# Two layers on one core: the merges' buffers and low parts, the last projection's banks, small matmuls of S5 and SSD, and how S5's time steps are loaded

## The chip, the core and the metric

The kernel runs on one core of a Trainium2 chip. The core has five engines with instruction streams of their own: TensorE (PE; its weight loads are listed as PEld), VectorE (DVE), ScalarE (ACT), GpSimd (POOL) and SyncE (SP), whose queue starts most DMAs here. The metric is the time of one execution on the device in microseconds; the figure to beat or miss is the median of three runs. A profiled execution gives the trace from which all rows below are taken.

## The reference, cut to what matters

The program computes two layers over 1024 tokens of width 1024, each of which projects its normalised input to three mixers and three gates, and merges the mixers' outputs.

```python
# layer 1: mixers S5 (a), mLSTM (b), sparse attention (c), each 512 wide
proj = rmsnorm(x, norm_g) @ w_in
y_a = s5_mixer(u_a, ...) * silu(z_a); y_b = mlstm(...) * silu(z_b); y_c = dsa(...) * silu(z_c)
branch = einsum('blnw,nwd->blnd', stack([y_a, y_b, y_c], 2), w_branch)
x1 = rmsnorm(x + sum(sigmoid(gate_pre) * branch, axis=2) @ w_out, final_norm_g)
# s5_mixer, 32 groups of 16 channels with 64 complex states each
dt = exp(log_dt)[:, None];  abar = exp(ar * dt) * (cos(ai * dt) + 1j * sin(ai * dt))
h[t] = abar * h[t - 1] + (bbar @ u[t]);  y = real(c @ h) + d_skip * u
# layer 2: stick-breaking attention (512), SSD (1024), RWKV-7 (512), merged in the same way
y_diag = einsum('bclgn,bcsgn,bcgjls,bcsgjp->bclgjp', cm, bm, decay_in, x_dt)     # SSD, chunks of 128
y_off = einsum('bclgn,bcgjpn,bcgjl->bclgjp', cm, prev_states, exp(a_cs))
out = rms_norm(x1 + sum(gate * (y @ w_out_i)) @ w_o, final_g)
```

## The kernel before

All tiles hold channels on the 128 partitions and tokens along the row. The large products are in three parts: each fp32 operand is split into a high part (a ScalarE copy to the engine's rounded fp32 type) and a low part (the rest, by VectorE or GpSimd), and `mm3` issues high x high, high x low and low x high as three matmuls of 128x128 by 512 columns, 0.227 us apart at the full clock. `proj` does one output tile of 128 channels in two halves of 512 tokens, each with a PSUM bank `pp` of its own (two banks in turn), and then calls an evacuation.

The order on each engine is fixed when the program is built: the scheduler of the tile framework lays out the instructions of all stages along its own time line, and each engine then runs its stream in order. Projections that a later stage needs (`ahead`: gates and values of the mixers, weights `fhi`/`flo`, written to DRAM through `fs`) are laid as fillers between the small matmuls of the recurrent stages.

Layer 1 runs norm, S5, sparse attention, mLSTM, merge, output projection with the norm of layer 2. Layer 2 runs the stick-breaking attention, SSD, RWKV-7, merge, output projection.

S5 (`s5`) reads its parameters, among them the 32 time steps, into `s5_dt` (two groups of 64 partitions by 16), takes their exponential (L583), and makes powers of the transition on VectorE. Then it goes through four channel tiles `ct`: the projection `uT` (evicted by ScalarE at L717), a convolution with a kernel `KK` of eight steps, held as the Toeplitz tile `Tz`, and a carry over blocks of eight tokens, a scan on VectorE that ends in `wr`/`wi`. The output of each of eight groups is Tz by U (128 rows) plus Vr by wr and Vi by wi (64 rows each, the upper or the lower half of the partitions), added up in PSUM.

SSD goes through eight chunks; for each half j of the heads it multiplies `xd` by `aB` (the part inside the chunk) and the state `S` by `bc` (the part from before).

A merge (`merge_branch`) goes through branches. `merge_y` loads the mixer's output y (and, where it is still to be gated, z), multiplies and splits it into the high and low tile in `hT[0]`. For each of eight output tiles d and each half, `eb` loads the gate `sg`, and VectorE multiplies it with the projection's bank (L425); GpSimd adds it to `acc` (L426). In layer 1 the branches run in the order a, c, b; in layer 2 four calls do attention, the two halves of SSD, and RWKV. The last branch does one half of the tokens after the other: behind its eight tiles, ScalarE writes the high part of the sum into `hT[0]` (L434) and VectorE the low part into `ml` (L435). `out_norm` then takes 128 tokens at a time: two PSUM banks `on` of 24 matmuls each, the residual `on_x` added by VectorE (L471), and the final norm.

The buffers of a merge are in one pool with two buffers a name: y has four, z two, the gate two; in layer 2 z takes the gate's.

Of the kernel before, what the change touches and what calls it, by code (L numbers as in the profile page):

```python
# [8 lines left out]
F32 = mybir.dt.float32  # L9
# [6 lines left out]
OP = mybir.AluOpType  # L16
# [93 lines left out]
def layout(i):  # L110
# [15 lines left out]
    o["s5_ldt"] = i["ssm_log_dt"][0]  # L126
# [52 lines left out]
class Kernel:  # L179
# [211 lines left out]
    def merge_y(self, p2, ysrc, zname, ztag, halves, here):  # L391
# [18 lines left out]
    def merge_branch(self, p2, first, last, acc, ysrc, zname, wb, base, gate, between=None, ml=None,  # L410
                     here=None, ztag="mg_z"):
# [3 lines left out]
        for halves in ((0,), (1,)) if last else ((0, 1),):  # L415
            y = self.merge_y(p2, ysrc, zname, ztag, halves, here)
            for d in range(8):
                def eb(half, ps):
                    t = slice(512 * half, 512 * half + 512)
                    sg = p2.tile([128, 512], F32, name="mg_s")  # L420
                    SP.dma_start(sg, self.done[f"{gate}_{d}"][:, t])
                    if first:
                        V.scalar_tensor_tensor(acc[:, d, t], sg, 1.0, ps, op0=OP.add, op1=OP.mult)
                    else:
                        V.scalar_tensor_tensor(sg, sg, 1.0, ps, op0=OP.add, op1=OP.mult)  # L425
                        self.G.tensor_tensor(acc[:, d, t], acc[:, d, t], sg, op=OP.add)  # L426
# [25 lines left out]
    def out_norm(self, ml, ws, res, g_dram, sm, done):  # L452

        tc, V, A, SP = self.tc, self.V, self.A, self.SP
        with self.pool(name="on", bufs=1) as pg, self.pool(name="on2", bufs=2) as p2, \
                self.pool(name="onp", bufs=2, space=PSUM) as pp:
# [22 lines left out]
    def block1(self):  # L479
# [3 lines left out]
        with ExitStack() as top:  # L483
# [59 lines left out]
            with self.pool(name="mw", bufs=2, side="right") as self.wp, \  # L543
                    self.pool(name="mg2", bufs=2, side="right") as p2:
# [19 lines left out]
            self.out_norm(ml, ws, I["x"], I["final_norm_g"], so, done)  # L564

    def s5(self, es):
# [129 lines left out]
        for ct in range(4):  # L696
# [60 lines left out]
            kks = [self.pm.tile([128, 4, 16], F32, name="pm") for _ in range(2)]  # L757
            for j in range(4):
                for g2 in range(2):
                    r = slice(64 * g2, 64 * g2 + 64)  # L760
                    self.mm(kks[g2][:, j], WTr[r, j].rearrange("p s q -> p (s q)"),
                            P["cr"][r, 4 * ct + j], True, False)
                    self.mm(kks[g2][:, j], WTi[r, j].rearrange("p s q -> p (s q)"),
                            nci[r, 4 * ct + j], False, True)
# [38 lines left out]
            yps = [self.pm.tile([128, 4, 128], F32, name="pm") for _ in range(2)]  # L803
            for j in range(4):
                for g2 in range(2):
                    g, ps = 2 * j + g2, yps[g2]
                    r = slice(64 * g2, 64 * g2 + 64)
# [521 lines left out]
    def block2(self):  # L1329
# [3 lines left out]
        with ExitStack() as top:  # L1333
# [36 lines left out]
            with self.pool(name="mw2", bufs=2, side="right") as self.wp, \  # L1370
                    self.pool(name="mg4", bufs=2, side="right") as p2:
# [737 lines left out]
```

## Time and profile before

| what | value |
|---|---|
| runs | 2820.71, 2817.85, 2813.22 us; median 2817.85 |
| profiled execution | 2822.19 us, span 2820.2, mean granted clock 0.977 |
| TensorE | 2687.4 us busy, 95% |
| VectorE, ScalarE, GpSimd | 1758.6 (62%), 1140.9 (40%), 660.9 us (23%) |
| DMA | 324.85 MB, 115 GB/s on average |

The profile is one execution. The span is the time from the first to the last instruction, and 2 us of the execution lie around it. The granted clock is TensorE's, 1 for 2.4 GHz and 0.5 for 1.2 GHz. In the rows, names are cut (`s_dt` for `s5_dt`, `hl` for the tile that is `acc` in a merge, since they share a buffer), and one fp32 matmul that is not split is two instructions.

### The profile page before, as it was taken

The numbers are of one execution on the slowest core, as the hardware profiler recorded it, in microseconds if no ns is written. First come the engines' busy times: TensorE is split into PE (matmuls) and PEld (weight loads), VectorE is DVE, ScalarE is ACT, GpSimd is POOL, SyncE is SP. The second block draws the span as 40 slices with busy tenths as digits, with TensorE's granted clock in tenths as the row PEclk, the third lists the DMA queues.
The fourth block names the chain that finished last, engine by engine and source line by source line (L and its number), as shares of the span: only waits on it lengthen the run. The fifth ranks groups of instructions, "written<-read, shape, count | busy, mean of one in ns | idle before, by whom it ended". The sixth has DMA issues, their size and how long they took to land. (4 is left out here: it accounts for less than half of the span.)

```text
span 2820.2 us, 40796 instructions
## 1 busy us (share of the span) xinstructions
PE 2687.4 (95%) x15464; PEld 2148.5 (76%) x15464; DVE 1758.6 (62%) x3439; ACT 1140.9 (40%) x2015; POOL 660.9 (23%) x507
## 2 busy tenths in 40 slices
PE   5999999999999998999999999999999999898988
PEld 4787888888888776777767777777777877686767
DVE  5976338899543776428857756564457364867562
ACT  3222336667333333237776634223324233422230
POOL 3112212122110034222211122344222221114420
PEclk8999999999999999999999999999999999899999
DMA  4333412222111755332232244433633232645352
GB/s 139 89 93 113 139 42 83 68 95 101 64 61 61 273 194 179 110 79 52 59 112 67 67 144 144 153 121 123 211 127 114 83 113 83 191 131 152 122 168 90
DMA packets 184876, 324.85 MB, mean 115 GB/s; under 512 B 47704, under 2 KB 74968, under 8 KB 183656
## 3 DMA queue, kind: packets, MB, share of 16 engines
q1 hardware_dynamic: 178344, 310.11, 34.3%
q0 software_dynamic: 5184, 7.93, 1.5%
q10 hardware_dynamic: 1152, 4.19, 0.4%
q8 instruction: 122, 2.00, 0.3%
q14 instruction: 74, 0.61, 0.1%
HBM read 218.10 MB, written 95.03 MB: 111 GB/s over the span
## 5 line engine op out<-in xcount | busy, mean ns | idle before, releaser
L173 PE MATMUL pp<-hh,fhi 128*128 128x512 f32 x1984 | 791.1, 399 | 15.0 <-ACT fs L317 9.5
L173 PE MATMUL pp<-hl,fhi 128*128 128x512 f32 x1984 | 786.9, 397 | 2.1 <-DVE hl L219 2.1
L173 PE MATMUL pp<-hh,flo 128*128 128x512 f32 x1984 | 786.4, 396 | 0.0
L330 POOL TENSOR_TENSOR flo<-fraw,fhi 128x1024 fp32r<-128x1024 f32 x124 | 315.3, 2542 | 965.0 <-ACT fhi L329 848.7
L173 PEld LDWEIGHTS pp<-hh,fhi 128*128 128x128 f32 x1984 | 374.2, 189 | 103.6 <-ACT fs L317 11.9
L173 PEld LDWEIGHTS pp<-hl,fhi 128*128 128x128 f32 x1984 | 374.5, 189 | 82.7 <-issue 3.3
L173 PEld LDWEIGHTS pp<-hh,flo 128*128 128x128 f32 x1984 | 373.9, 188 | 82.0 <-issue 4.2
L173 PE MATMUL pp<-hh,whi 128*128 128x512 f32 x976 | 332.0, 412 | 34.9 <-ACT s_uT L717 14.9
L173 PEld LDWEIGHTS pp<-hh,whi 128*128 128x128 f32 x976 | 185.7, 194 | 84.9 <-ACT s_uT L717 15.8
L173 PE MATMUL pp<-hh,wlo 128*128 128x512 f32 x528 | 214.5, 406 | 2.3 <-DVE wlo L219 2.3
L329 ACT ACTIVATE fhi<-fraw 128x1024 fp32r<-128x1024 f32 x124 | 130.1, 1049 | 176.9 <-PE pp L173 127.0
L426 POOL TENSOR_TENSOR hl<-hl,mg_s 128x512 f32<-128x512 f32 x80 | 125.4, 1568 | 176.6 <-DVE mg_s L425 174.6
L218 ACT ACTIVATE whi<-wraw 128x512 fp32r<-128x512 f32 (+2 forms) x87 | 58.9, 678 | 178.1 <-PE pp L173 140.9
L173 PEld LDWEIGHTS pp<-hh,wlo 128*128 128x128 f32 x528 | 103.1, 195 | 26.8 <-DVE wlo L219 4.5
L269 ACT ACTIVATE fs<-pp 128x512 f32<-128x512 f32 x128 | 75.5, 590 | 116.7 <-issue 56.0
L173 PE MATMUL on<-on_wh,hh 128*128 128x512 f32 x256 | 102.7, 402 | 13.6 <-DVE on_x L471 12.4
L173 PE MATMUL on<-on_wl,hh 128*128 128x512 f32 x256 | 101.9, 398 | 0.4 <-DVE on_wl L219 0.4
L173 PE MATMUL on<-on_wh,ml 128*128 128x512 f32 x256 | 101.7, 398 | 0.0
L425 DVE SCALAR_TENSOR_TENSOR mg_s<-mg_s,pp 128x512 f32<-128x512 f32 x80 | 54.5, 681 | 55.1 <-PE pp L173 32.5
L219 DVE TENSOR_TENSOR wlo<-wraw,whi 128x512 fp32r<-128x512 f32 (+2 forms) x87 | 73.6, 848 | 23.5 <-ACT whi L218 23.3
L1450 DVE TENSOR_SCALAR sb_e<-sb_z 128x512 f32<-128x512 f32 (+3 forms) x96 | 51.8, 548 | 46.7 <-PE sb_z L173 46.2
L1453 DVE TENSOR_TENSOR sb_e<-sb_e,sb_z 128x512 f32<-128x512 f32 (+3 forms) x96 | 51.5, 546 | 32.6 <-ACT sb_e L1452 32.3
(675 smaller groups left out, 4768.5 us busy)
## 6 DMA issues: line engine op xcount, KB each, us to landing
fraw<-in_w_in_dram SPq DMA_DIRECT2D x123, 512.0 KB, 3.6
mg_s<-ahead_g SPq DMA_DIRECT2D x112, 256.0 KB, 3.2
ahead_g<-fs SPq DMA_DIRECT2D x96, 256.0 KB, 2.0
wraw<-in_w_branch_dram SPq DMA_DIRECT2D x32, 256.0 KB, 3.2
sd_aB<-sd_ad SPq DMA_DIRECT2D x8, 1024.0 KB, 5.7
mg_y<-y2d SPq DMA_DIRECT2D x30, 256.0 KB, 4.1
mg_y<-yd SPq DMA_DIRECT2D x24, 256.0 KB, 4.5
xin<-in_x_dram SPq DMA_DIRECT2D x8, 512.0 KB, 5.6
```

Source lines behind the costliest of these rows:

```text
L173: self.issued(self.pe.matmul(*a, **k))
L218: self.A.activation(hi, src, AF.Copy)
L219: (eng or self.V).tensor_tensor(lo, src, hi.bitcast(F32), op=OP.subtract)
L269: return self.A.activation(out, x, AF.Tanh, **k)
L329: self.A.activation(hi, raw, AF.Copy)
L330: self.G.tensor_tensor(lo, raw, hi.bitcast(F32), op=OP.subtract)
L425: V.scalar_tensor_tensor(sg, sg, 1.0, ps, op0=OP.add, op1=OP.mult)
L426: self.G.tensor_tensor(acc[:, d, t], acc[:, d, t], sg, op=OP.add)
L1450: V.tensor_scalar(e, z, 40.0, None, op0=OP.min)
L1453: V.tensor_tensor(e, e, z, op=OP.max)
```

## The change

Five things change. The time steps come from the host as 128 rows of 16 numbers, and one DMA (L582) takes the place of two that read one number per descriptor with strides. In S5, Tz by U of all eight groups is issued first, and then Vr of group 2j, Vr of 2j+1, Vi of 2j, Vi of 2j+1, so that neighbours use different halves of the rows and different banks; KK is written in the same manner. In SSD the products with S are issued together, alternating j in the code, and then all products of xd. In the merges y, z and the gate share one name with a ring of eight slots (layer 1) or six (layer 2), and in the last branch the low part is made within `eb`, tile by tile: ScalarE copies the high part into the gate's slot (L430), VectorE subtracts it (L431), and ScalarE still writes `hT[0]` at the end (L439). The last output projection has four banks instead of two.

```diff
-    o["s5_ldt"] = i["ssm_log_dt"][0]
+    o["s5_ldt"] = c(np.repeat(i["ssm_log_dt"][0].reshape(16, 2).T, 64, axis=0))
...
-        ldt = I["s5_ldt"]
-        for g2 in range(2):
-            SP.dma_start(dt[64 * g2:64 * g2 + 64],
-                         bass.AP(tensor=ldt.tensor, offset=ldt.offset + g2, ap=[[0, 64], [2, 16]]))
+        SP.dma_start(dt, I["s5_ldt"])
...
+            for g in range(8):
+                self.mm(yps[g % 2][:, g // 2], Tz[:, g].rearrange("p t q -> p (t q)"), U[:, g], g < 2, False)
             for j in range(4):
-                for g2 in range(2):
-                    g, ps = 2 * j + g2, yps[g2]
-                    r = slice(64 * g2, 64 * g2 + 64)
-                    self.mm(ps[:, j], Tz[:, g].rearrange("p t q -> p (t q)"), U[:, g], True, False)
-                    self.mm(ps[:, j, 1:], Vr[r, j].rearrange("p t q -> p (t q)"), wr[r, j, 0:127], False, False)
-                    self.mm(ps[:, j, 1:], Vi[r, j].rearrange("p t q -> p (t q)"), wi[r, j, 0:127], False, True)
+                for x, y in ((Vr, wr), (Vi, wi)):
+                    for g2, r in enumerate(halves):
+                        self.mm(yps[g2][:, j, 1:], x[r, j].rearrange("p t q -> p (t q)"), y[r, j, 0:127],
+                                False, j == 3 and x is Vi)
...
-                    y = p2.tile([128, 512], F32, name="mg_y", bufs=4)
+                    y = p2.tile([128, 512], F32, name="mg_y", tag="mg")
...
-                    z = p2.tile([128, 512], F32, name="mg_z", tag=ztag)
+                    z = p2.tile([128, 512], F32, name="mg_z", tag="mg")
...
-                    sg = p2.tile([128, 512], F32, name="mg_s")
+                    sg = p2.tile([128, 512], F32, name="mg_s", tag="mg")
...
+                    if last:
+                        self.A.activation(sg.bitcast(F32R), a, AF.Copy, scale=0.5)
+                        V.scalar_tensor_tensor(ml[:, d, t], a, 0.5, sg, op0=OP.mult, op1=OP.subtract)
...
                     self.A.activation(self.hT[0][:, d, t], acc[:, d, t], AF.Copy, scale=0.5)
-                    V.scalar_tensor_tensor(ml[:, d, t], acc[:, d, t], 0.5, self.hT[0][:, d, t].bitcast(F32),
-                                           op0=OP.mult, op1=OP.subtract)
...
-                    self.pool(name="mg2", bufs=2, side="right") as p2:
+                    self.pool(name="mg2", bufs=8, side="right") as p2:
...
-                    self.pool(name="mg4", bufs=2, side="right") as p2:
+                    self.pool(name="mg4", bufs=6, side="right") as p2:
...
-            self.out_norm(ml, ws, self.x1, I["final_g_2"], sm, done)
+            self.out_norm(ml, ws, self.x1, I["final_g_2"], sm, done, 4)
...
+                for k in range(4):
+                    for j in range(2):
+                        r = slice(64 * j, 64 * j + 64)
+                        self.mm(yo[j][:, k], S[r, 2 * k:2 * k + 2].rearrange("p h e -> p (h e)"), bc[r, 1, t],
+                                True, True)
...
+            for h in range(16):
+                self.mm(yds[h // 8][64 * (h % 2):64 * (h % 2) + 64, h // 2 % 4], xd[:, h], aB[:, h], True, True)
```

Since the scheduler lays out the whole program anew, the order on every engine changes in S5, mLSTM with the first merge, the attention of layer 2, SSD, and RWKV with the second merge; the sparse attention's stays. In SSD the rows have four products of S with j = 0, four with j = 1, then sixteen of xd, where they had eight, four, eight, four. At the end of RWKV 20 filler matmuls, which stood behind it, now stand ahead of the matmuls on `rw_w`.

On TensorE, in S5's first channel tile, the output matmuls stood in turns of Tz, Vr and Vi for each group (`pm_787` and `pm_788` are the two banks), in the kernel before:

```order
L173 MATMUL pm_787<-s5_U_633,s5_Tz_744 128x128
L173 MATMUL pm_787<-s5_wr_764,s5_Vr_670 128x127
L173 MATMUL pm_787<-s5_wi_765,s5_Vi_671 128x127
L173 MATMUL pm_788<-s5_U_633,s5_Tz_744 128x128
L173 MATMUL pm_788<-s5_wr_764,s5_Vr_670 128x127
L173 MATMUL pm_788<-s5_wi_765,s5_Vi_671 128x127
```

The same place in the changed kernel (banks `pm_786` and `pm_787`):

```order
L173 MATMUL pm_786<-s5_wi_764,s5_Vi_670 128x127
L173 MATMUL pm_787<-s5_wi_764,s5_Vi_670 128x127
L173 MATMUL pm_786<-s5_wr_763,s5_Vr_669 128x127
L173 MATMUL pm_787<-s5_wr_763,s5_Vr_669 128x127
L173 MATMUL pm_786<-s5_wi_764,s5_Vi_670 128x127
L173 MATMUL pm_787<-s5_wi_764,s5_Vi_670 128x127
```

Tz is gone from between them; its eight matmuls stand 60 rows earlier in one run, and Vr and Vi now take the two banks, and with them the two halves of the rows, in turn.

On SyncE's queue, around the passage from the first branch of merge 1 to the second, the kernel before has the second branch's inputs (`yd2`, `ahead_zc`) among the first gates (`mg_s` from `ahead_g0`):

```order
L402 DMA mg_y_9081<-yd2_93 128x512
L421 DMA mg_s_8834<-ahead_g0_1_6679 128x512
L405 DMA mg_z_8772<-ahead_za3_5727 128x512
L405 DMA mg_z_9083<-ahead_zc0_5792 128x512
L402 DMA mg_y_9088<-yd2_93 128x512
L1033 DMA yd1_92<-ml_z_8274 128x1024
L402 DMA mg_y_9095<-yd2_93 128x512
L405 DMA mg_z_9090<-ahead_zc1_5857 128x512
L405 DMA mg_z_9097<-ahead_zc2_5922 128x512
L1024 DMA ml_z_8411<-ahead_zb1_5337 128x1024
L402 DMA mg_y_9102<-yd2_93 128x512
L957 DMA ml_k_8564<-ml_k3_6546 128x1024
```

In the changed kernel they begin behind the first branch's last gates (`ahead_g0_7`):

```order
L422 DMA mg_s_9039<-ahead_g0_6_6993 128x512
L289 DMA wraw_9004<-in_w_branch_dram 128x512
L422 DMA mg_s_9061<-ahead_g0_7_7056 128x512
L958 DMA ml_vt_8429<-ahead_v2_5145 128x1024
L422 DMA mg_s_9077<-ahead_g0_7_7056 128x512
L289 DMA wraw_9042<-in_w_branch_dram 128x512
L402 DMA mg_y_9080<-yd2_93 128x512
L405 DMA mg_z_9082<-ahead_zc0_5791 128x512
L289 DMA wraw_9136<-in_w_branch_dram 128x512
L1032 DMA yd1_92<-ml_z_8410 128x1024
L402 DMA mg_y_9087<-yd2_93 128x512
L1023 DMA ml_z_8547<-ahead_zb2_5401 128x1024
```

What moved is the y and z of the next branch: from ahead of the gates of d = 1 to behind those of d = 7.

On TensorE, at the end of the merge of layer 2, the kernel before has these rows from the last projection (`pp_23497`) on, where `on_23547` and `on_23573` are the first two banks of the output projection and `on_23607` the next:

```order
L173 MATMUL pp_23497<-hh_63,whi_23492 128x512 x2
L173 MATMUL pp_23497<-hh_63,wlo_23493 128x512
L173 MATMUL on_23547<-on_wh0_21969,hh_63 128x512
L173 MATMUL on_23547<-on_wl0_21970,hh_63 128x512
L173 MATMUL on_23547<-on_wh0_21969,ml_21973 128x512
L173 MATMUL on_23573<-on_wl1_21972,hh_63 128x512
L173 MATMUL on_23573<-on_wh1_21971,ml_21973 128x512
L173 MATMUL on_23573<-on_wh1_21971,hh_63 128x512
L173 MATMUL on_23573<-on_wl1_21972,hh_63 128x512
L173 MATMUL on_23573<-on_wh1_21971,ml_21973 128x512
L173 MATMUL on_23607<-on_wh0_21969,hh_63 128x512
L173 MATMUL on_23607<-on_wl0_21970,hh_63 128x512
```

In the changed kernel, the last matmuls before the third bank, `on_23698`; 24 rows on `on_23638` and `on_23664` stand between the last projection and it:

```order
L173 MATMUL on_23664<-on_wh1_21986,ml_21988 128x512
L173 MATMUL on_23664<-on_wh1_21986,hh_63 128x512
L173 MATMUL on_23664<-on_wl1_21987,hh_63 128x512
L173 MATMUL on_23664<-on_wh1_21986,ml_21988 128x512
L173 MATMUL on_23664<-on_wh1_21986,hh_63 128x512
L173 MATMUL on_23664<-on_wl1_21987,hh_63 128x512
L173 MATMUL on_23664<-on_wh1_21986,ml_21988 128x512
L173 MATMUL on_23698<-on_wh0_21984,hh_63 128x512
L173 MATMUL on_23698<-on_wl0_21985,hh_63 128x512
L173 MATMUL on_23698<-on_wh0_21984,ml_21988 128x512
```

So 24 matmuls instead of eight separate the last projection from the third bank's first matmul.

## Rows read from the trace of the kernel before

**Rows 1.** The page, part 1: busy time, share of the span, instructions.

```profile
PE 2687.4 (95%) x15464; PEld 2148.5 (76%) x15464; DVE 1758.6 (62%) x3439; ACT 1140.9 (40%) x2015; POOL 660.9 (23%) x507
```

**Rows 2.** Waits of PE, whole span: awaited group: us in total, times, longest us.

```profile
PE pp L173 <- ACT s_uT L717: 15.2, 3, 12.2
PE on L173 <- DVE on_x L471: 12.4, 2, 6.3
...
PE pp L173 <- DVE mg_s L425: 11.4, 15, 2.1
```

**Rows 3.** The tile s_dt: issues (ns each, first and last start us) and landing.

```profile
L581 SPq DMA_DIRECT2D s_dt<-in_s_ldt_dram x2: 662/704/747, 39.2 to 40.0; - x2
...
DMA to landing us min/median/max: 12.6/16.5/20.3
```

**Rows 4.** DMA issues from 0 to 130 us: count, KB each, us to landing.

```profile
s_ar<-in_s_ar_dram SPq DMA_DIRECT2D x1, 8.0 KB, 4.8
...
glub<-in_glu_b_dram SPq DMA_DIRECT2D x1, 2.0 KB, 1.8
```

**Rows 5.** Timeline from 60 us: start, us, engine, operation; idle before, releaser.

```profile
60.41 0.21 ACT L583 ACTIVATE s_dt<-s_dt 128x16 f32<-128x16 f32 x1 [25.78 <-DMA s_dt<-in_s_ldt_dram]
...
63.59 0.79 PE L173 MATMUL pp<-hh,whi 128*128 128x512 f32 x1 [12.22 <-ACT s_uT L717]
```

**Rows 6.** Windows of ten us: busy us by engine, granted clock, DMA, GB/s.

```profile
50.00:60.00 10.00, 1.37 (x6) 0.78 (x5) 0.00 (x0) 0.00 (x0) 0.00 (x0) 0.71 0.05 0
60.00:70.00 10.00, 5.86 (x16) 4.36 (x16) 8.50 (x62) 4.26 (x9) 3.40 (x14) 0.61 0.13 53
70.00:80.00 10.00, 8.46 (x40) 6.09 (x41) 10.00 (x71) 0.00 (x0) 0.00 (x0) 0.73 0.33 81
...
2430.00:2440.00 10.00, 8.93 (x139) 5.78 (x139) 8.01 (x15) 2.60 (x5) 3.37 (x2) 0.50 0.77 251
```

**Rows 7.** Timeline of PE from 112.9 us, S5 of the first channel tile.

```profile
112.94 0.49 PE L173 MATMUL pm<-s_U,s_Tz 128*128 128x128 f32 x2
113.36 0.48 PE L173 MATMUL pm<-s_wr,s_Vr 64*128 64x127 f32 x2
113.68 0.38 PE L173 MATMUL pm<-s_wi,s_Vi 64*128 64x127 f32 x2
114.00 0.49 PE L173 MATMUL pm<-s_U,s_Tz 128*128 128x128 f32 x2
```

**Rows 8.** Groups by form, PE: form, count, busy us, mean ns, idle before.

```profile
L173 PE MATMUL op<-d_pT,d_v 128*128 128x128 f32 x288 | 38.1, 280 | 1.5 <-ACT d_pT L1318 1.5
```

**Rows 9.** Timeline of PE, two places in SSD.

```profile
1772.55 0.49 PE L173 MATMUL pm<-sd_bc 64*128 64x128 f32 x4
1772.97 1.09 PE L176 MATMUL pm<-ident,sd_xs 128*128 128x128 f32 x8
...
1783.52 1.16 PE L173 MATMUL pm<-sd_bc,sd_S 64*128 64x128 f32 x8
1784.60 0.33 PE L176 MATMUL pm<-ident,sd_bc 128*128 128x128 f32 x1
```

**Rows 10.** Timeline of PE from 935 us, start of the first merge.

```profile
935.51 0.79 PE L173 MATMUL pp<-hh,whi 128*128 128x512 f32 x1 [3.35 <-ACT hh L218]
937.68 0.80 PE L173 MATMUL pp<-hh,whi 128*128 128x512 f32 x1 [1.38 <-DVE hh L219]
```

**Rows 11.** Waits of PE from 1020 to 1100 us, first merge.

```profile
PE pp L173 <- DVE mg_s L425: 7.5, 8, 2.1
```

**Rows 12.** The page, parts 5 and 6: two merge groups, one DMA issue.

```profile
L426 POOL TENSOR_TENSOR hl<-hl,mg_s 128x512 f32<-128x512 f32 x80 | 125.4, 1568 | 176.6 <-DVE mg_s L425 174.6
...
L425 DVE SCALAR_TENSOR_TENSOR mg_s<-mg_s,pp 128x512 f32<-128x512 f32 x80 | 54.5, 681 | 55.1 <-PE pp L173 32.5
...
mg_y<-yd SPq DMA_DIRECT2D x24, 256.0 KB, 4.5
```

**Rows 13.** Timeline of PE at the end of rwkv.

```profile
2421.96 1.87 PE L173 MATMUL op<-rw_bo,rw_w 128*128 128x2 f32 x8 [2.29 <-ACT rw_w L2049]
```

More of the change, by code (lines that the diff above doesn't have):

```diff
@@ L388, in bcast_row, with merge_y @@
         return t
-    def merge_y(self, p2, ysrc, zname, ztag, halves, here):
+    def merge_y(self, p2, ysrc, zname, halves, here):
         yh, yl = self.hT[0][:, 0::2], self.hT[0][:, 1::2]
@@ L410, in merge_branch @@
     def merge_branch(self, p2, first, last, acc, ysrc, zname, wb, base, gate, between=None, ml=None,
-                     here=None, ztag="mg_z"):
+                     here=None):
         V, SP = self.V, self.SP
         for halves in ((0,), (1,)) if last else ((0, 1),):
-            y = self.merge_y(p2, ysrc, zname, ztag, halves, here)
+            y = self.merge_y(p2, ysrc, zname, halves, here)
             for d in range(8):
@@ L450, in out_weights, with out_norm @@
         return ws, load
-    def out_norm(self, ml, ws, res, g_dram, sm, done):
+    def out_norm(self, ml, ws, res, g_dram, sm, done, banks):
         tc, V, A, SP = self.tc, self.V, self.A, self.SP
         with self.pool(name="on", bufs=1) as pg, self.pool(name="on2", bufs=2) as p2, \
-                self.pool(name="onp", bufs=2, space=PSUM) as pp:
+                self.pool(name="onp", bufs=banks, space=PSUM) as pp:
             mh = self.hT[0]
@@ L757, in s5 @@
             kks = [self.pm.tile([128, 4, 16], F32, name="pm") for _ in range(2)]
+            halves = [slice(0, 64), slice(64, 128)]
             for j in range(4):
-                for g2 in range(2):
-                    r = slice(64 * g2, 64 * g2 + 64)
[L761 to L764, printed above, removed]
+                for x, y in ((WTr, P["cr"]), (WTi, nci)):
+                    for g2, r in enumerate(halves):
+                        self.mm(kks[g2][:, j], x[r, j].rearrange("p s q -> p (s q)"), y[r, 4 * ct + j],
+                                x is WTr, x is WTi)
             for g2 in range(2):
@@ L803, in s5 @@
             yps = [self.pm.tile([128, 4, 128], F32, name="pm") for _ in range(2)]
+            for g in range(8):
+                self.mm(yps[g % 2][:, g // 2], Tz[:, g].rearrange("p t q -> p (t q)"), U[:, g], g < 2, False)
             for j in range(4):
-                for g2 in range(2):
-                    g, ps = 2 * j + g2, yps[g2]
-                    r = slice(64 * g2, 64 * g2 + 64)
-                    self.mm(ps[:, j], Tz[:, g].rearrange("p t q -> p (t q)"), U[:, g], True, False)
-                    self.mm(ps[:, j, 1:], Vr[r, j].rearrange("p t q -> p (t q)"), wr[r, j, 0:127], False, False)
-                    self.mm(ps[:, j, 1:], Vi[r, j].rearrange("p t q -> p (t q)"), wi[r, j, 0:127], False, True)
+                for x, y in ((Vr, wr), (Vi, wi)):
+                    for g2, r in enumerate(halves):
+                        self.mm(yps[g2][:, j, 1:], x[r, j].rearrange("p t q -> p (t q)"), y[r, j, 0:127],
+                                False, j == 3 and x is Vi)
             for g2 in range(2):
@@ L1376, in block2 @@
                     self.merge_branch(p2, j == 0, j == 3, acc, self.yd2[j], z, I[w], base, f"g{g}", load, ml,
-                                      self.rw_y if j == 3 else None, "mg_s")
+                                      self.rw_y if j == 3 else None)
             def done(i, y):
                 SP.dma_start(self.out[128 * i:128 * i + 128], y)
-            self.out_norm(ml, ws, self.x1, I["final_g_2"], sm, done)
+            self.out_norm(ml, ws, self.x1, I["final_g_2"], sm, done, 4)
     def sb(self, es):
@@ L1584, in ssd @@
                 A.activation(eA, eA, AF.Exp)
-            for j in range(2):
-                yd = self.pm.tile([128, 4, 128], F32, name="pm")
-                for k in range(4):
-                    for g in range(2):
-                        h = 2 * (4 * j + k) + g
-                        self.mm(yd[64 * g:64 * g + 64, k], xd[:, h], aB[:, h], True, True)
-                if c:
-                    yo = self.pm.tile([128, 4, 128], F32, name="pm")
-                    r = slice(64 * j, 64 * j + 64)
-                    for k in range(4):
-                        self.mm(yo[:, k], S[r, 2 * k:2 * k + 2].rearrange("p h e -> p (h e)"), bc[r, 1, t],
-                                True, True)
-                    e = eA[:, 4 * j:4 * j + 4]
-                    V.tensor_tensor(e, yo, e, op=OP.mult)
+            if c:
+                yo = [self.pm.tile([128, 4, 128], F32, name="pm") for _ in range(2)]
+                for k in range(4):
[3 more added lines that the diff above has]
+                                True, True)
+                for j in range(2):
+                    e = eA[:, 4 * j:4 * j + 4]
+                    V.tensor_tensor(e, yo[j], e, op=OP.mult)
+            yds = [self.pm.tile([128, 4, 128], F32, name="pm") for _ in range(2)]
+            for h in range(16):
+                self.mm(yds[h // 8][64 * (h % 2):64 * (h % 2) + 64, h // 2 % 4], xd[:, h], aB[:, h], True, True)
+            for j in range(2):
+                yd = yds[j]
                 for k in range(4):
@@ L1603, in ssd @@
                 if c:
-                    G.tensor_tensor(xs[:, 4 * j:4 * j + 4, t], xs[:, 4 * j:4 * j + 4, t], e, op=OP.add)
+                    G.tensor_tensor(xs[:, 4 * j:4 * j + 4, t], xs[:, 4 * j:4 * j + 4, t], eA[:, 4 * j:4 * j + 4],
+                                    op=OP.add)
             if c < 7:
```

7 lines of the change are left out of this document (4 added, 3 removed).

## The prediction

> **What bounds the kernel now.** The page's first part comes first: TensorE is busy for 2687.4 us of 2820.2 [rows 1], so 133 us are idle, and nothing that leaves TensorE's own work alone can bring more than that and the time lost at the low clock. VectorE (62%), ScalarE and GpSimd have room on average, so the question is which waits TensorE has, and where it issues slower than it could. The table of TensorE's waits comes next [rows 2]: the longest that the change touches are one of 12.2 us on `s_uT` (15.2 us in three waits), two on the result of the output projection (12.4 us in all) and fifteen on the gated tile `mg_s` (11.4 us). TensorE takes its instructions in the order of the program, and the projections of later stages ("fillers") are laid between the small matmuls; a wait on one small result therefore stops all of it, and behind a long wait comes a stretch at the lower of its two clocks, 1.2 GHz. In the windows behind the first wait the granted clock is 0.61 and 0.73 of 2.4 GHz [rows 6]: 5.86 us x 0.39 and 8.46 us x 0.27, or 2.3 us each, are lost beside the wait itself.
>
> **The time steps (`s5_ldt`).** The two element-wise DMAs of L581 are issued at 39.2 and 40.0 us and take up to 20.3 us to land [rows 3]. The exponential waits for them until 60.41 us, having been idle for 25.78 us, and because ScalarE's queue is in order, the eviction `s_uT` (L717) behind it holds TensorE until 63.59 us [rows 5]. The change reads 128 rows of 64 bytes in one DMA. The nearest rows are the other small parameters of S5, which are contiguous rows too: 1.8 us (`glub`) to 4.8 us (`s_ar`) to landing [rows 4]. So the exponential runs at about 39.2 + 2.3 = 41.5 us, 19 us earlier, and no ScalarE or VectorE work stands in that stretch to push it back. The VectorE chain of the first channel tile (8.5 and 10 us busy in the windows from 60 to 80 [rows 6]) moves with it. TensorE has fillers until 63.59 - 12.2 = 51.4 us, and what it can gain is the idle time and the lost clock: 12.2, 2.3, 2.3, and the other two waits of the same kind, 3.0 us together with another 2 to 3 us of clock behind the later one. That is a cap of 22. I take 18, with 16 (the wait and the clock of the two windows behind it) and 22 as ends.
>
> **S5's output matmuls.** For each of 8 groups the kernel before issues Tz on 128 rows, then Vr and Vi on 64 rows: starts at 112.94, 113.36, 113.68 and the next group at 114.00 [rows 7], or 0.42 + 0.32 + 0.32 = 1.06 us, 8.46 us for each of four channel tiles. Alone, a 128x128 by 128 matmul of this type costs 38.1 / 288 = 0.132 us per instruction [rows 8], so a Tz (two instructions) would cost 0.26 in a run: 0.16 of its 0.42 is the change between the two shapes. After the change the 8 Tz stand in one run: 16 x 0.132 = 2.1 us. Vr and Vi alternate row halves. The row that shows alternate row halves at nearly this size is `sd_bc` by `sd_bc`: four instructions in 0.42 us [rows 9], of which up to 0.16 is the change of shape, so 0.065 to 0.105 each; on one row half eight take 1.08 us, 0.135 each [rows 9]. With 0.08, 32 instructions are 2.6 us; the sum is 2.1 + 2.6 + 0.1 = 4.8, against 8.46: 3.7 us less per channel tile. Ends: 0.135 (no overlap) gives 6.5 and a gain of 2.0, 0.065 gives 4.2 and 4.2.
> The Trainium skill (TensorEngine Tiling (Array Packing), Theoretical Speedup and Key Properties) says that a contraction of up to 64 rows can run up to twice as fast on two row tiles, and that changing the tiling mode drains the engine. By that 0.0675 us an instruction and 4.3 us a tile would be the figure; the row's 0.105 with its change of shape neither excludes nor proves it, so I stay between.
> For channel tiles 2 to 4 TensorE is full (from 140 us on), so the whole 3 x 3.7 = 11 us count (6 to 12.6). In the first, TensorE waits for the VectorE chain; Tz has left the path there (the first order excerpt), which shortens the path behind `wi`, but the cap above is shared: 3.5 (0 to 6). The KK matmuls already alternate in the kernel before: nothing.
>
> **SSD.** Per chunk two changes of shape go (0.05 to 0.16 us each by [rows 7]), over 7 chunks 0.7 to 2.2 us; but the S matmuls stand as four and four on one row half each, so no overlap is added. I take 2 (0 to 5, if TensorE's wait for the VectorE product goes as well).
>
> **Merge of block 1.** At its start TensorE waits 3.35 and 1.38 us for split inputs [rows 10], because the z of k = 2 and 3 have only two buffers and are loaded late; with eight slots all are loaded in a row: 4.7 less, and up to 2.5 of clock. The gate waits, 7.5 us in eight [rows 11], come from two gate buffers; with eight slots the gate is there, and what is left is VectorE's own lag: 5 of the 7.5. Against it stands the queue (second order excerpt): y and z of the next branch now stand behind all gates of the present one, and y and z of k = 3 take the slots of the last two gates. These come free when the last gate has been consumed: 0.68 (L425) + 1.57 (POOL, L426) + 4.5 (y to landing) [rows 12] + 0.6 + 0.7 for the split = 8.1 us behind the last projection, of which the k = 0 to 2 matmuls of the first tile (18 x 0.227 = 4.1 us in two halves) cover half: 4 us, and 2 to 3 of clock. In the kernel before, those loads are ahead of the gates. I count 6.7 for it in block 1, where mLSTM matmuls stand beside the first boundary: 4.7 + 5 - 6.7 = 3 less (14 less to 6 more). The low parts tile by tile give nothing here: ScalarE still writes `hT` (L434 before, L439 after) for d = 0 to 5 ahead of the last two copies, and with two banks the first of the two waits for `on_x` (12.4 - 6.3 = 6.1 us) stays. The 32 added ScalarE copies, 0.63 us each, are 20 us on an engine that is 40% busy.
>
> **Merge of block 2.** The remaining gate waits, 11.4 - 7.5 = 3.9 [rows 2, 11], go to 3 less; the three boundaries cost 3 to 4 as above where no filler is left (rwkv fills most). At the end the second of the two waits for `on_x`, 6.3 us [rows 2], goes: 24 output matmuls (5.4 us) now stand behind the last projection before the next bank, eight before (third excerpt), and banks three and four give as many again while VectorE catches up; with it goes a stretch of low clock, 2.3 us by the windows behind the first wait [rows 6]. I take 5.3 + 2.3, since the matmuls after the 24 still need the last gated tile off its bank. Sum 3 + 7.6 - 3.5 = 7 less (13 less to 2 more).
>
> **End of rwkv.** Ahead of 2421.96 us TensorE waits 2.29 us for `rw_w`, and the small matmuls behind it run at a clock of 0.50 in the window from 2430 [rows 6, 13]: 8.93 x 0.5 = 4.5 us are lost there and, by my estimate, about as much from 2420 to 2430. In the new order 20 fillers stand ahead of that wait. It may go whole (11) or be replaced by another (5 more); I take 5 less.
>
> **The sum.** 18 + 3.5 + 11 + 2 + 3 + 7 + 5 = 49.5. The profiled execution took 2822.2 us, so 2772.7 on its own time; the median of the runs is 4.3 us under it: 2768.
>
> **Rivals.**
> First, S5 alone gains: row halves don't overlap (2 a tile, 6 for three) and the first tile's matmuls give nothing, 18 + 6 = 24, SSD 2, and what the deep ring gives is handed back at the branch boundaries: 26 less, 2792 on the median. For it: the 0.105 of [rows 9] is not far from 0.135, and the order at the boundary. Against it: 5 to 9 us of known waits are simply gone at the end of block 2.
> Second, everything comes at its better end, also the clock: dt 22, S5 5 and 12, SSD 4, merges 12 and 11, rwkv 9 = 75 less, 2743.
> Third, slower: the shared ring. All seven passages from one branch or half to the next (three in block 1, four in block 2) lose the whole 8.1 us and 2.5 of clock, 74 us; the end of rwkv moves 5 the other way; the sure gains of S5 (24) and of the bank and gates (7.6 + 8) stand against it: 79 - 40 = 39 slower, 2857. It decides from about 6 us a passage. Against it: TensorE has the fillers' or the recurrent layer's matmuls beside five of the seven.
> That the change doesn't do what it says holds for SSD alone, whose matmuls don't alternate in the order; it is worth 2 us and is in the ranges.
>
> **How the numbers follow.** Forecast (2750 to 2785) 0.5; first rival 0.23; second 0.18; third, weakened or whole, 0.09. The 0.3% that a measurement of this kernel can tell is 8.5 us. The third rival's mild form (4 to 6 us a passage) is no change, 0.04, its full form slower, 0.05; all else is faster, 0.91. The ends of all terms together give 2733 and 2809; 8 in 10 lie in 2737 to 2798.
>
> **What would show it.** Right: `s_dt` lands by 42 us and the wait on `s_uT` is under 3 us; ten-us windows from 50 to 130 have TensorE at 9 or more; the Vr and Vi rows start 0.16 us a pair, not 0.27; a channel tile lasts 3 to 4 us less; no wait for `on_x` in block 2 and the same 6 us in block 1; `mg_s` waits under 4 us, and new waits on `hh` at the boundaries, under 5 us each. Wrong: VectorE's chain in the first channel tile doesn't move, as something else holds its start; Vr and Vi at 0.135 an instruction; waits of 8 us or more where a branch begins; or a longer stretch at 1.2 GHz in rwkv, where the order of the fillers has changed for other reasons than the merge.

## The result, and the profile after

The changed kernel takes 2777.72 us (median of four runs, 2773.34 to 2787.0) against 2818.2: a ratio of 0.9863, 95% interval 0.9834 to 0.9891, or 39 us less (31 to 47). In a later job, beside other kernels and on one chip with them, it was 2776.35, a ratio of 0.984 (0.9827 to 0.9853). The forecast was 2768 in a range of 2737 to 2798, so time and sign were right. The experiments show that the sum came out right with several of its terms wrong, so its closeness is in part luck.

The first part of the page of the changed kernel; 114.6 us of TensorE are idle, 18 fewer than in [rows 1]:

```profile
PE 2657.0 (96%) x15455; PEld 2126.0 (77%) x15464; DVE 1760.8 (64%) x3439; ACT 1157.8 (42%) x2047; POOL 659.8 (24%) x507
```

TensorE's waits in the changed kernel, whole span (us in total, times, longest), beside [rows 2]: `s_uT` and `mg_s` have fallen to 4.6 and 4.8 us, but one of the two waits for `on_x` has grown to 9.1.

```profile
PE on L173 <- DVE on_x L474: 9.5, 2, 9.1
...
PE pp L173 <- DVE mg_s L427: 4.8, 6, 1.7
PE pp L173 <- ACT s_uT L717: 4.6, 3, 2.2
```

The time steps, tile `s_dt` of the changed kernel (issue, then the exponential, with first and last start): one DMA at 38.7 us, in use at 40.5, where [rows 3, 5] had 60.4.

```profile
L582 SPq DMA_DIRECT2D s_dt<-in_s_ldt_dram x1: 429/429/429, 38.7 to 38.7; - x1
L583 ACT ACTIVATE s_dt<-s_dt x1: 216/216/216, 40.5 to 40.5; 128x16 f32<-128x16 f32 x1
```

Ten-us windows of the changed kernel, columns as in [rows 6]: TensorE is full at 2.4 GHz from 50 to 80 us. VectorE is now busy for 9.77 to 10 of 10 us, and from 80 us on TensorE has gaps again.

```profile
50.00:60.00 10.00, 10.00 (x60) 7.63 (x59) 10.00 (x71) 1.54 (x2) 0.00 (x0) 1.00 0.42 131
60.00:70.00 10.00, 10.00 (x73) 7.74 (x72) 9.77 (x74) 3.46 (x7) 0.21 (x1) 1.00 0.13 33
70.00:80.00 10.00, 10.00 (x54) 8.57 (x53) 9.77 (x22) 2.15 (x4) 3.41 (x2) 1.00 0.39 125
80.00:90.00 10.00, 9.34 (x44) 7.10 (x42) 9.95 (x15) 2.15 (x3) 2.50 (x1) 1.00 0.34 113
90.00:100.00 10.00, 8.48 (x53) 6.40 (x53) 10.00 (x65) 1.77 (x4) 0.00 (x0) 0.83 0.34 54
```

S5's output matmuls in the changed kernel, timeline of TensorE: the sixteen Tz instructions take 1.70 us (74.07 to the next start at 75.77), and in a run four Vr or Vi instructions on alternate row halves follow each other at 0.22 to 0.23 us, 0.056 each, where [rows 7] had 0.16 each and [rows 9] 0.135 on one half.

```profile
74.07 1.95 PE L173 MATMUL pm<-s_U,s_Tz 128*128 128x128 f32 x16
75.77 0.48 PE L173 MATMUL pp<-hh,fhi 128*128 128x512 f32 x1
...
90.91 0.39 PE L173 MATMUL pm<-s_wr,s_Vr 64*128 64x127 f32 x4
91.13 0.39 PE L173 MATMUL pm<-s_wi,s_Vi 64*128 64x127 f32 x4
91.35 0.39 PE L173 MATMUL pm<-s_wr,s_Vr 64*128 64x127 f32 x4
```

The start of the first merge, timeline of the changed kernel: 0.55 and 1.72 us of wait, where [rows 10] has 3.35 and 1.38.

```profile
910.87 0.51 PE L173 MATMUL pp<-hh,whi 128*128 128x512 f32 x1 [0.55 <-ACT hh L218]
...
913.10 0.50 PE L173 MATMUL pp<-hh,whi 128*128 128x512 f32 x1 [1.72 <-DVE hh L219]
```

**Where the time went.** Since the whole layout moves, a stage's time means little without the fillers that ran in it. The table gives, for each kernel and mark, the time of the mark less that of the kernel before (profiled executions), less 0.227 us for each 512-column projection matmul (`pp`) that it has done more by then: work done early is no loss. Negative is ahead of the kernel before. "Changed" is the profile of the later job.

| mark | rows alone | S5 alone | merges alone | SSD alone | rows + SSD | changed |
|---|---|---|---|---|---|---|
| S5's last output | -18.7 | -4.6 | -2.4 | -1.7 | -17.7 | -28.2 |
| sparse attention's last transpose | -19.2 | -4.3 | -2.4 | -1.3 | -16.9 | -29.9 |
| mLSTM's last transpose | -18.6 | -2.8 | 3.6 | 0.8 | -15.4 | -20.1 |
| first `on_x` of block 1 | -17.6 | -3.2 | 3.2 | 0.2 | -16.2 | -18.5 |
| SSD's first product | -14.7 | -4.0 | 7.6 | -2.2 | -22.4 | -22.7 |
| SSD's last product | -14.4 | -3.7 | 7.0 | -4.2 | -23.6 | -23.0 |
| first `rw_GT` | -12.3 | -2.5 | 4.0 | -8.3 | -24.7 | -24.8 |
| last `rw_GT` | -11.5 | -1.9 | 1.4 | -16.3 | -31.5 | -36.4 |
| last `on_x` | -12.3 | 1.5 | -7.2 | -15.8 | -30.6 | -46.3 |

A profiled execution is up to 11 us off its kernel's median in these jobs (merges alone: 2814.8 against 2825.65), so a step of 2 or 3 us in the table says nothing; the ratios below decide, and the table says where. The first profile of the changed kernel and those of the four runs that start from it in one job lack the records of nine projection matmuls (x15455 of PE beside x15464 of PEld in the page above); the figures given for them below count these nine in, 2.0 us from the sparse attention's end on.

### The profile page after: what moved, and what is told of

Read it like the earlier page. It is cut to its first block, busy times and chain, and to the rows that moved or that the text cites. A ratio compares the mean times of both kernels' runs of the same rounds, so it can differ in the third digit from the quotient of the medians.

```text
span 2771.6 us, 40828 instructions
## 1 busy us (share of the span) xinstructions
PE 2657.0 (96%) x15455; PEld 2126.0 (77%) x15464; DVE 1760.8 (64%) x3439; ACT 1157.8 (42%) x2047; POOL 659.8 (24%) x507
## 5 line engine op out<-in xcount | busy, mean ns | idle before, releaser
L173 PE MATMUL pp<-hh,whi 128*128 128x512 f32 x976 | 323.7, 403 | 14.2 <-DVE mg_s L427 4.8
L173 PEld LDWEIGHTS pp<-hh,wlo 128*128 128x128 f32 x528 | 100.0, 189 | 28.2 <-DVE wlo L219 7.4
L427 DVE SCALAR_TENSOR_TENSOR mg_s<-mg_s,pp 128x512 f32<-128x512 f32 x80 | 54.4, 682 | 39.5 <-PE pp L173 30.0
```

The lines of the kernel that those rows point to most:

```text
L173: self.issued(self.pe.matmul(*a, **k))
```

## The experiments

The first four each add one part of the change to the kernel before, in one job (before: 2821.97 us).

**The rows of time steps alone.**

```diff
+        SP.dma_start(dt, I["s5_ldt"])
```

> The kernel before with the time steps loaded as rows, nothing else. The prediction's term: 18 us less (16 to 22), 2800 us. If the gain needs the shorter output matmuls too, or something else holds the first channel tile, under 12 us.

2805.38 us, ratio 0.9935 (0.9922 to 0.9948): 18 us less (15 to 22). The whole gain is there at S5's last output. The term stands as it was.

**S5's matmuls alone** (Tz first, Vr and Vi alternating, KK too).

```diff
+            for g in range(8):
+                self.mm(yps[g % 2][:, g // 2], Tz[:, g]..., U[:, g], g < 2, False)
...
+                for x, y in ((Vr, wr), (Vi, wi)):
+                    for g2, r in enumerate(halves):
```

> The kernel before with S5's matmuls in the new order, nothing else. If TensorE is full in channel tiles 2 to 4, as the prediction said, 14 us less or, with the 0.056 us an instruction of the trace after, up to 18. If the tiles are then held by the chain through VectorE (the next tile's uT waits for the last reader of this tile's), as the trace after suggests, 3 to 7 us less, and TensorE has new waits on s_uT there.

2822.94 us, ratio 1.001 (0.9999 to 1.0022): nothing gained. Waits of TensorE from 80 to 260 us in this kernel, then two 20-us windows, of the kernel before first and then of this one:

```profile
PE pp L173 <- ACT s_uT L717: 6.5, 3, 2.9
PE pm L176 <- DVE s_WTr L618: 4.2, 4, 1.4
```

```profile
160.00:180.00 20.00, 20.00 (x126) 15.69 (x125) 18.93 (x92) 4.45 (x9) 3.48 (x1) 1.00 0.32 80
...
220.00:240.00 20.00, 19.68 (x111) 15.99 (x110) 16.85 (x58) 7.90 (x13) 0.43 (x1) 1.00 0.47 136
```

```profile
160.00:180.00 20.00, 16.08 (x114) 12.99 (x111) 20.00 (x86) 6.00 (x11) 2.39 (x1) 0.96 0.42 106
...
220.00:240.00 20.00, 15.57 (x90) 12.01 (x89) 13.57 (x35) 6.18 (x8) 3.31 (x2) 1.00 0.35 112
```

In the kernel before TensorE had been full there; now it waits some 4 us of 20 in these two windows, most of it for `s_uT`, the next channel tile's input, which comes through the chain on VectorE and ScalarE. What its shorter matmuls free becomes idle time: 4.6 us ahead at the end of S5, not 14, and nothing of it is left in the time.

**The merges alone** (ring, low parts, four banks).

```diff
+                    y = p2.tile([128, 512], F32, name="mg_y", tag="mg")
...
+                    if last:
+                        self.A.activation(sg.bitcast(F32R), a, AF.Copy, scale=0.5)
...
+            self.out_norm(ml, ws, self.x1, I["final_g_2"], sm, done, 4)
```

> The kernel before with the merges' ring, low parts and four banks, nothing else. The prediction's terms (merge 1, merge 2, end of rwkv): 15 us less. By the stages of the two traces: 15 to 20 less, with the wait for on_x in the first merge longer than in the kernel before (9 instead of 6 us), and gone in the second.

2825.65 us, ratio 1.0008 (0.9995 to 1.0021): nothing, against 15 expected. The table shows two halves of opposite sign: 6 us lost between the sparse attention and the end of mLSTM, where merge 1's first branches run, 4 more by SSD's first product, and 9 won at the end, in merge 2. The wait for `on_x` in the first merge was 9.4 us, the second 0.3. This profile is the fastest of its twelve runs, 11 us under their median, so the table shows this kernel at its best.

**SSD alone.**

```diff
+                for k in range(4):
+                    for j in range(2):
+                        self.mm(yo[j][:, k], S[r, ...], bc[r, 1, t], True, True)
...
+            for h in range(16):
+                self.mm(yds[h // 8][...], xd[:, h], aB[:, h], True, True)
```

> The kernel before with SSD's matmuls grouped, nothing else. The prediction's term: 2 us less (0 to 5). The stages of the two traces show some 5 us less between the attention's end and SSD; if these come from the grouping, 5 to 8 less; if from a new layout, nothing or a loss.

2807.92 us, ratio 0.9954 (0.9942 to 0.9966): 13 us less (10 to 16), more than either theory allowed. In SSD itself the table shows 2 us, as predicted. But the layout runs 76 fewer filler matmuls by SSD's last product (5794 against 5870), and 48 more in RWKV's last part. The 512-column matmuls (columns: length, PE and PEld busy, then VectorE, ScalarE, clock, DMA share, GB/s) from the first to the last `rw_GT`, first in the kernel before, then with SSD grouped:

```profile
2213.90:2658.80 444.90, 291.02 (x1123) 209.13 (x1123) 32.68 (x48) 13.68 (x23) 0.96 0.42 127
```

```profile
2194.70:2642.50 447.80, 299.62 (x1171) 214.74 (x1171) 32.70 (x48) 14.82 (x25) 0.98 0.42 128
```

48 more (10.9 us of work) run in 2.9 us more time. They stand ahead of the matmuls on `rw_w` that waited 2.29 us in [rows 13]; here these start without a wait, and behind them the clock is low (0.58) in one window of ten us, and at 0.91 in the next, where [rows 6] has 0.50. Up to these matmuls both kernels have run the same 7488 projection matmuls; what is laid differently is that 577 of them come behind the first `rw_GT`, where it was 529.

```profile
2414.77 0.72 PE L173 MATMUL gb<-rw_DT,rw_TX 32*32 32x32 f32 x19
2415.41 1.87 PE L173 MATMUL op<-rw_bo,rw_w 128*128 128x2 f32 x8
```

The next four start from the changed kernel, in one job (before: 2824.93 us).

**uT and U uncoupled.** This kernel leaves S5's skip term out.

```diff
-            V.scalar_tensor_tensor(yt, uT, P["d"][:, ct:ct + 1], yt, op0=OP.mult, op1=OP.add)
-            sq = w2.tile([128, 8, 128], F32, name="sq", tag="s5_U")
+            V.scalar_tensor_tensor(yt, yt, P["d"][:, ct:ct + 1], yt, op0=OP.mult, op1=OP.add)
+            sq = w2.tile([128, 8, 128], F32, name="sq", tag="s5_Tz")
```

> The changed kernel with two couplings between S5's channel tiles taken away: the skip term reads yt in the place of uT (so the output leaves out the skip term of S5; the instruction and its time are the same), and sq uses the slot of Tz instead of U's. If the next tile's uT and U, each with a single buffer, hold TensorE in channel tiles 2 to 4, the waits on s_uT there go and the time falls by 6 to 11 us. If VectorE's own work is the bound (about 40 of 47 us a tile), 0 to 3 us.

2798.94 us, ratio 0.9903 (0.9882 to 0.9925): slower than the changed kernel. What the theory named is in the changed kernel's trace, the last reader of one tile's uT, in VectorE's queue, and behind it the eviction of the next tile's and TensorE (ScalarE's `sq`, which waits for the same reader, stands ahead of that eviction):

```profile
153.79 1.28 DVE L818 SCALAR_TENSOR_TENSOR yt<-s_uT,s_d,yt 128x1024 f32<-128x1024 f32 x1
155.10 1.06 ACT L820 ACTIVATE sq<-yt 128x1024 f32<-128x1024 f32 x1 [7.03 <-DVE yt L818]
156.06 1.07 ACT L717 ACTIVATE s_uT<-pp 128x512 f32<-128x512 f32 x2
156.69 0.19 PEld L173 LDWEIGHTS pp<-hh,whi 128*128 128x128 f32 x1 [2.39 <-ACT s_uT L717]
156.69 0.50 PE L173 MATMUL pp<-hh,whi 128*128 128x512 f32 x1 [1.97 <-ACT s_uT L717]
```

With the coupling gone the waits on `s_uT` are gone too, and VectorE is busy for 19.9 and 20.0 of 20 us in the first two windows:

```profile
60.00:80.00 20.00, 20.00 (x123) 16.24 (x122) 19.91 (x101) 5.15 (x10) 1.20 (x1) 1.00 0.18 57
80.00:100.00 20.00, 20.00 (x153) 16.30 (x153) 19.97 (x92) 5.46 (x11) 0.00 (x0) 1.00 0.44 116
```

But TensorE is idle for longer, 19.4 us from 60 to 240 us where the changed kernel has 11.8. It now waits for the evictions of fillers (`fs`) and for `s_yd` (waits from 60 to 240 us):

```profile
PE pp L173 <- ACT fs L317: 6.7, 2, 5.8
PE pp L173 <- DVE fs L315: 5.8, 1, 5.8
PE pm L173 <- DMA s_yd<-s_yg: 4.2, 1, 4.2
```

S5's last output came at 228.2 us instead of 236.5 (in the kernel with `on_x` apart of the same job), but with 62 fewer projection matmuls behind it (597 against 659, 14 us), and RWKV's last part lost its gain (16.8 us ahead at the last `rw_GT`, the changed kernel 36.4). So the coupling was one hold, others of the same size stand close behind it, and why RWKV loses is open.

**on_x apart.**

```diff
+            px = top.enter_context(self.pool(name="onx", bufs=2))
...
-                x = p2.tile([128, D], F32, name="on_x")
+                x = (px or p2).tile([128, D], F32, name="on_x")
```

> The changed kernel with the residual tiles on_x of block 1 in two buffers of their own beside the merge's, so that their loads need not wait for a slot of the ring. If that load sets the wait of 9.07 us at the end of merge 1, the wait falls to 3 us or less and the time by 6 to 9 us, with the low clock behind it 8 to 11. If the two banks or the writing of the high parts set it, as the prediction said, it stays at 6 to 9 us.

2776.57 us, ratio 0.9828 (0.9815 to 0.9841). First the changed kernel at the end of merge 1 (timeline): the loads of `on_x` are issued at 1105.32 us, and VectorE waits 4.80 us for them, TensorE 9.07.

```profile
1104.94 0.33 SPq L387 DMA_DIRECT2D on_g<-in_final_norm_g_dram  x1
1105.32 0.90 SPq L467 DMA_DIRECT2D on_x<-in_x_dram  x2
...
1110.55 1.29 DVE L474 TENSOR_TENSOR on_x<-on,on_x 128x512 f32<-128x512 f32 x2 [4.80 <-DMA on_x<-in_x_dram]
1111.30 0.80 PE L173 MATMUL on<-on_wh,hh 128*128 128x512 f32 x1 [9.07 <-DVE on_x L474]
```

Its SP queue's waits from 1095 to 1112 us say why: the load of `on_g` (L387), which stands just ahead of `on_x` on that queue, waits 16.4 us for the low part (L431) that frees a slot of the ring, whose memory the output stage takes over.

```profile
SPq L387 <- DVE ml L431: 16.4, 1, 16.4
```

With two buffers apart the first load is at 1014.3 us, and no wait for `on_x` is left in either block:

```profile
L467 SPq DMA_DIRECT2D on_x<-in_x_dram x8: 327/328/424, 1014.3 to 1171.8; - x8
```

The cause is shown: at the first `on_x` this kernel is 31.4 us ahead, the changed one 18.5 to 21.1. In the time little of it is left: at SSD's first product it is 26.8 ahead against 22.7 to 25.8, and the two ratios lie in each other's reach. The changed kernel makes up 8 us between the end of the stick-breaking attention and SSD's first product (17.8 to 25.8 ahead, first profile), where this one stays; what holds SSD's start for both is open.

**The old buffers.**

```diff
+                    y = p2.tile([128, 512], F32, name="mg_y", bufs=4)
+                    z = p2.tile([128, 512], F32, name="mg_z", tag=ztag)
+                    sg = p2.tile([128, 512], F32, name="mg_s")
```

> The changed kernel with the buffers of the merges as before (y four, z two, gate two, in block 2 z with the gate), low parts and banks as changed. If the ring gives what the prediction counted (first fill 4.7, gates 5 + 3, less 10 at the passages, and 5 at the end of rwkv): 3 to 8 us slower. If the passages eat it all: the same within 3 us; on_x in merge 1 loads earlier, so the wait there is shorter.

2782.36 us, ratio 0.9852 (0.9839 to 0.9864): 3 us slower than the changed kernel by the later job's 0.984, with intervals that overlap. From the sparse attention to mLSTM's end it loses nothing (25.4 to 25.2 ahead), where the changed kernel falls from 29.9 to 20.1 (first profile: 27.0 to 21.0); from the last `rw_GT` to the end it gains 1.5, the changed kernel 9.9. The waits in that last stretch:

```profile
PE pp L173 <- DVE mg_s L427: 8.1, 2, 7.1
```

and in the changed kernel, from 2600 to 2700 us:

```profile
PE on L173 <- DVE on_x L474: 0.5, 1, 0.5
...
PE pp L173 <- DVE mg_s L427: 0.3, 1, 0.3
```

So by the table the ring costs in merge 1 about what it gives in merge 2. But the wait of 7.1 us is not one of the kernel before, which has no wait for `mg_s` in that stretch: with two gate buffers the tile-by-tile low part, which sits in the gate's slot, holds up the next gate's load. Timeline of the old buffers, where L427 needs that gate at 2644.01 us:

```profile
2638.31 1.29 DVE L431 SCALAR_TENSOR_TENSOR ml<-hl,mg_s 128x512 fp32r<-128x512 f32 x2
...
2639.03 0.93 SPq L422 DMA_DIRECT2D mg_s<-ahead_g  x2
```

In part, then, the ring takes away a wait that the low parts bring.

**The low parts late.**

```diff
+                    V.scalar_tensor_tensor(ml[:, d, t], acc[:, d, t], 0.5, self.hT[0][:, d, t].bitcast(F32),
+                                           op0=OP.mult, op1=OP.subtract)
```

> The changed kernel with the low parts made at the end as before, ring and banks as changed. The prediction gave the tile-by-tile low parts nothing in block 1 and left block 2's gain to the banks: within 3 us, if on_x in merge 1 waits for its load anyway. If the low parts are what frees VectorE at the end of merge 2, 4 to 7 us slower, with a wait for on_x or on ml there.

2783.51 us, ratio 0.9856 (0.9842 to 0.9869): some 4 us slower than the changed kernel by 0.984, with intervals that overlap. From the last `rw_GT` to the end it gains 7.0 against 9.9. The waits for `on_x` are 6.5 and 2.9 us. The low parts are a small gain, if any.

The last four share a job (before: 2822.03 us).

**Time steps and SSD together** (the diffs of the first and the fourth).

> The kernel before with two parts, the time steps as rows and SSD's grouping. If these two carry the change and the rest is worth nothing: 28 to 34 us less (18 + 13), with the wait for rw_w at the end of RWKV gone. If S5's order and the merges are worth their part once the first two are there, the changed kernel in the same job is 5 to 12 us faster still.

2790.5 us, ratio 0.9885 (0.9869 to 0.99): 32 us less, the sum of the two alone. The changed kernel beside it had 0.984: S5's order and the merges, worth nothing alone, are worth 13 us on top of these two. By the table none of that is left ahead of the first `rw_GT`, where the two kernels are level (24.7 and 24.8): S5's 10 us pay for what merge 1 loses, and the gain comes in RWKV's last part (5) and in merge 2 (11). Which of the two parts is needed for it was not run.

**Fillers held back.**

```diff
-            ahead(*[f"g{n}_{d}" for n in range(3) for d in range(8)], gate="tanh")
+            ahead(*[f"g{n}_{d}" for n in range(3) for d in range(8)][:-1], "@mid1", "g2_7", gate="tanh")
```

> The kernel before, in which the last 12 of the 24 gate projections may not be laid before the first middle part of RWKV; nothing else. At the first rw_GT it then has as few fillers behind it as the kernel with SSD grouped (48 fewer). If fillers left over for the end of RWKV are the whole gain of the grouping, 8 to 13 us less. If the gain needs SSD's own chain to be shorter, what is won at the end of RWKV (8 to 12 us) is lost ahead of it, where TensorE now waits: within 4 us, and the front part of RWKV longer.

2822.6 us, ratio 1.0004 (0.9995 to 1.0012). The edit is not the one that the expectation names: it holds back one gate projection, the last of the 24 (`g2_7`), and only until the mark `@mid1`, not twelve until the first middle part. At the first `rw_GT` of the chain 6959 projection matmuls had run, as before, and 8082 at the last, as before, so nothing was left over for the end, and the wait for `rw_w` stayed at 2.3 us. So neither theory of SSD's gain was tested by it.

**The changed kernel again.**

> The changed kernel again, beside the others of this job. 1.4% faster than the kernel before (39 us, 31 to 47).

2776.35 us, ratio 0.984 (0.9827 to 0.9853), as given above.

**on_x apart, and the skip term in KK.**

```diff
-            V.scalar_tensor_tensor(yt, uT, P["d"][:, ct:ct + 1], yt, op0=OP.mult, op1=OP.add)
...
-                A.activation(KK[:, g2::2], kks[g2], AF.Copy)
+                V.tensor_tensor(KK[:, g2::2], kks[g2], dk[ct // 2][:, ct % 2, g2::2], op=OP.add)
```

> The changed kernel with on_x of block 1 in buffers of its own, and with S5's skip term put on the diagonal of the kernel KK (four VectorE passes of 1.28 us go, and uT is free once it is copied to DRAM; sq takes Tz's slot). By the experiments before: on_x 6 to 10 us less, S5 up to 8 less if the layout of the fillers stays: 2755 to 2765 us. If any edit in S5 moves the fillers out of RWKV's end, as when uT was uncoupled, that gives 10 to 15 back: 2768 to 2780.

2781.86 us, ratio 0.9862 (0.9841 to 0.9882): not better than the changed kernel. It is 10 us further ahead than that up to the first `rw_GT` (34.7 against 24.8) and has lost it at the end (32.5 against 46.3): in merge 2 TensorE waits 5.9 us for `on_x` and up to 4.2 us for `on_wh`, where the changed kernel's first profile has 0.5 and 1.1. The time is 2 us above the second case of the expectation, and no version was faster than the changed kernel. By the tables, the old buffers in block 1 with the ring in block 2 might be one; it was not run.

## Why the prediction was right, and which of its steps were not

**The time steps**: right in mechanism and size, 18 us predicted, 18 measured; the exponential starts 1.8 us after the issue, and the windows from 50 to 80 are full.

**S5's matmuls**: the step that failed is "TensorE is full (from 140 us on), so the whole 3 x 3.7 = 11 us count". The saving was larger than worked out: 1.7 us for Tz and 2.2 for Vr and Vi with their changes of shape, 3.9 in the place of 8.46 in the first tile, and over the four tiles the three groups' busy time fell from 38.9 to 21.1 us, 4.4 a tile where 3.7 had been counted. But a TensorE that is full says only that nothing else was late yet. The chain of one channel tile through VectorE (20 of 20 us busy in a window) was about as long, and alone the new order gave nothing. On top of the earlier start it shows as 10 us at S5's end (28.2 against 17.7 in one job), which merge 1 took back. The prediction had a page's rule beside this term: the Trainium skill (TensorEngine Tiling (Array Packing), Theoretical Speedup) says up to two times for a contraction of up to 64 rows; the rows here show 0.135 against 0.056 us, 2.4 times. The measurement decides; the operand shapes of the two differ by one column, and the faster ones also go into two banks in turn, which no run separates from the row halves.

**SSD**: a term of the sum that was mis-sized, 2 predicted, 13 measured. Its own stage gave the 2; most of the other 11 comes behind it, 8 of them in RWKV's last part, where the 48 filler matmuls that are no longer laid ahead of it fall into waits and low clock. That the gain comes there is shown by the two traces; that left-over fillers alone would bring it is argued, since the run meant to test it held back too little.

**The end of RWKV**: 5 us were counted, with 11 as the end, because fillers stood ahead of the wait for `rw_w` in the new order. That wait did go, and of the low clock, two windows at 0.50 before, one is left in the changed kernel (columns as in [rows 6]):

```profile
2397.00:2407.00 10.00, 10.00 (x88) 8.68 (x85) 5.51 (x11) 4.44 (x8) 4.03 (x2) 0.56 0.92 298
2407.00:2417.00 10.00, 8.71 (x73) 5.72 (x71) 9.98 (x20) 6.26 (x13) 0.71 (x2) 1.00 0.77 242
```

But it was SSD's grouping and not the merges that moved the fillers: with the merges alone the wait of 2.29 us is still there, with SSD alone it is gone.

**Merge 1**: 3 us less predicted, 6 to 11 us more measured from the sparse attention's end to the first `on_x` (merges alone 5.6, changed 11.4 and, in its first profile, 5.9; with the old buffers 3). The first waits, of 4.7 us, fell to 2.3, and the gate waits from 7.5 to 4.5, 3 us where 5 had been counted. The third rival's mechanism, and the 6.7 us counted for the passages, do not show: no wait for split inputs (`hh`) stands where the second or third branch begins. What grew instead, beside the wait for `on_x`, are waits that the kernel before and the old buffers do not have there, for the weights' low parts and of mLSTM's own matmuls (changed kernel, waits from 850 to 1120 us):

```profile
PE pp L173 <- DVE wlo L219: 3.0, 3, 1.5
PE pm L173 <- DVE ml_C L998: 2.0, 3, 1.5
...
PE pm L176 <- DVE ml_hn L1021: 1.2, 1, 1.2
PE pm L173 <- DVE ml_z L1029: 1.1, 1, 1.1
```

Why the ring brings them was not tried. The step on the wait for `on_x`, that it stays at 6 us for the two banks and the high parts, was wrong in its cause: the low parts tile by tile did free VectorE in time, and the wait grew to 9 us because the residual's load waits for the ring. No trace of the kernel before could show that; the pools' memory could have told it.

**Merge 2**: 7 less predicted, 9 to 10 measured (merges alone 8.6, changed 9.9), and the wait for `on_x` went from 6.3 to 0.5 us as said. The ring has its part in it, since with the low parts and without it a wait of 7.1 us for `mg_s` comes up there. The four banks were not tried by themselves.

**The sum**: 49.5 counted against 39 to 45. S5's order was put too high by 4 to 14 us and merge 1 by 9 to 14; SSD with the end of RWKV was too low by some 6, merge 2 by 2 to 3. The errors cancelled in part, and the range, built from the ends of each term, held; that the forecast lies within 10 us of the result is luck as much as reckoning. Of the signs that it named, the wait for `on_x` in block 1 (9.1 us, not 6) and those for `mg_s` (4.8 us, not under 4) failed.

## What to carry to other kernels

When one engine is full, find the next chain before counting its saved work as saved time: the time that the engine gains is bounded by how much later the next chain would have been. In a program with fillers, the value of a shorter stage lies where the fillers go that it no longer needs, so look for the last wait without cover. And when several names share one ring, look which memory the next stage takes over, since its loads then wait for the ring's last user.

## What was not expected of the hardware

Matmuls of 64 rows on alternate row halves, into different banks, followed each other at 0.056 us, against 0.135 for eight on one half ([rows 9]): more than twice as fast. Sixteen 128x128 by 128 matmuls in one run took 1.70 us, 0.106 each, where [rows 8] gives 0.132 on average.
